# Seven block products in place of eight in two of the eight chunks of the gate and up projections

## The chip, the cores and the metric

One core of one Trainium2 chip runs the whole layer. The metric is the device time of one execution in microseconds (us). Engines are named as in the profile: PE (TensorE, matmuls; PEld is its weight load), DVE (VectorE), ACT (ScalarE), POOL (GpSimd), SP (SyncE, which issues most DMAs).

## The reference

The reference is a one-layer encoder trunk on 256 tokens of width 2048 in float32: four mixers with gates, an output projection, and a SwiGLU feed-forward with norms around each part. The change touches the feed-forward alone:

```
h = rms_norm(x, norm_ffn_pre[l])                                        # 256 x 2048
ffn = (jax.nn.silu(h @ w_gate[l]) * (h @ w_up[l])) @ w_down[l]          # 2048 -> 5632 -> 2048
x = x + rms_norm(ffn, norm_ffn_post[l])
```

## The kernel before

A float32 product is made as three products in the fp32r type. Each operand is split into a rounded part hi and a rest lo, and the kernel adds hi x hi, hi x lo and lo x hi. The activations are split once (`h2_hi`, `h2_lo`, features on partitions, 16 k tiles of 128 features x 256 tokens). The weights are split as they arrive.

The weights are streamed in chunks of 256 features x 512 columns (512 KB). `Stream.chunk` (L588 to L602) loads a chunk by a DMA of SP into a `raw` tile (4 buffers, L592 and L593), ACT rounds it into `hi` (L600), and DVE subtracts to get `lo` (L601); `hi` and `lo` have 3 buffers each. These instructions carry a high scheduling priority, so they run as far ahead of the matmuls as the buffers allow.

`gemm_tok` (L646 to L664) multiplies 256 tokens by 512 columns. It goes through eight chunks; for each of a chunk's two k tiles and two halves of 128 tokens it issues three matmuls (L661 to L663), with the tokens as the stationary operand and 512 weight columns as the moving one. That makes 12 matmuls of 512 columns per chunk and 96 per projection, which accumulate in two PSUM banks. `gemm_feat` (L669 to L683), used earlier in the layer and not touched, is the other way round: its matmuls move 256 columns.

The feed-forward goes through 11 pairs (loop over `g`, L1019): a gate projection, a sigmoid on ACT and a product on DVE for each token half (L1025, L1026), an up projection, a product of the two on DVE (L1029), eight transposes on PE into `tq` (L1034), and two copies to `aT` on ACT (L1035). After the pairs comes the down projection (L1039 to L1088). Its activations are split per chunk into `ah` on ACT (L1044) and `al` on DVE (L1045), three buffers each, and its matmuls are L1056 to L1058. Half of its PSUM banks come from a pool `wd`, opened after the pool `tq` is closed (L1036). `ah`, `al`, `fg`, `sq` and `gain` lie in the pool `F`, which is open from before the first pair. The row of gains for the last norm is loaded by a DMA of POOL before the first pair (L1017).

The program is traced in this order and then scheduled by the framework: each engine gets one queue in order, by priority and by the framework's own estimate of when operands are ready, and semaphores are put where an operand or a buffer is needed. Engines carry out their queues in order.

Of the kernel before, what the change touches and what calls it, by code (L numbers as in the profile page):

```python
# [581 lines left out]
class Stream:  # L582


    def __init__(self, e, ring):
        self.e, self.ring = e, ring
# [18 lines left out]
def hybrid_kernel(tc, x, xt, w_l, w_in, w_branch, w_out, w_gate, w_up, w_down, post_mix, post_ffn, wa2_d, w2_d, a2_d, g2_d, lq_d,  # L605
                  vec_d, cst_d, lev_d, out):
    from contextlib import ExitStack
    nc = tc.nc
    V, S, G, T = nc.vector, nc.scalar, nc.gpsimd, nc.tensor
    e = Env()  # L610
    e.tc, e.nc = tc, nc
    e.boost, e.mix, e.nraw, e.nhi = 200000, 100000, 4, 3
    mm = T.matmul

    with ExitStack() as ctx:
        base = ctx.enter_context(tc.tile_pool(name="base", bufs=1))
        ring = ctx.enter_context(tc.tile_pool(name="ring", bufs=1))
# [2 lines left out]
        e.dram = ctx.enter_context(tc.tile_pool(name="dr", bufs=1, space=bass.MemoryType.DRAM))  # L620
        mmp = ctx.enter_context(tc.tile_pool(name="mmp", bufs=1, space=PSUM))
        stream = Stream(e, ring)

        def bank():
            return mmp.tile([128, 512], F32, tag="mm", name="mm", bufs=4)
# [15 lines left out]
        def rms(ssum, n, eps):  # L641

            V.tensor_scalar(ssum, ssum, 1.0 / n, eps, op0=ALU.mult, op1=ALU.add)  # L643
            G.tensor_tensor(ssum, ssum, e.mhalf.to_broadcast(list(ssum.shape)), op=ALU.pow)

        def gemm_tok(w, lhs, nk, banks, runs={}, into={}):  # L646
# [92 lines left out]
        with ExitStack() as mctx:  # L739
# [54 lines left out]
            with ExitStack() as rctx:  # L794
# [32 lines left out]
                for q, c0 in (("l", None), ("k", COL["rk"]), ("r", COL["rr"]), ("v", COL["rv"])):  # L827
# [4 lines left out]
                    if q == "l":  # L832
# [3 lines left out]
                        o = VCOL["w0"][0]  # L836
# [40 lines left out]
            with ExitStack() as sctx:  # L877
# [6 lines left out]
                k = e.M.tile([128, 2, 256], F32, tag="m2", name="k")  # L884
# [5 lines left out]
                for c in range(2):  # L890
                    t = e.M.tile([128, 2, 512], F32, tag="m4", name="vg")
# [121 lines left out]
        with ExitStack() as fctx:  # L1013
            F = fctx.enter_context(tc.tile_pool(name="F", bufs=1))
            aT = F.tile([128, 44, 256], F32, name="aT")
            gain = F.tile([128, 2048], F32, name="gain2")
            nc.gpsimd.dma_start(gain, post_ffn.unsqueeze(0).to_broadcast([128, 2048]))  # L1017
            with tc.tile_pool(name="tq", bufs=1, space=PSUM) as tq:
                for g in range(11):  # L1019
                    bg, bu = [bank(), bank()], [bank(), bank()]  # L1020
                    lhs2 = lambda kt: (h2_hi[:, kt], h2_lo[:, kt])
                    sg = F.tile([128, 2, 512], F32, tag="sg", name="sg", bufs=2)
                    gemm_tok(columns(w_gate, g), lhs2, 16, bg, {0: 3} if g == 0 else {})
                    for i in range(2):
                        S.activation(sg[:, i], bg[i], AF.Sigmoid, scale=r2[:, i, 0:1])  # L1025
                        V.scalar_tensor_tensor(sg[:, i], bg[i], r2[:, i, 1:2], sg[:, i], op0=ALU.mult, op1=ALU.mult)  # L1026
                    gemm_tok(columns(w_up, g), lhs2, 16, bu)
                    for i in range(2):
                        V.tensor_tensor(sg[:, i], sg[:, i], bu[i], op=ALU.mult)  # L1029
                    for kp in range(2):  # L1030
                        ps = tq.tile([128, 2, 256], F32, tag="tq", name="tq", bufs=4)
                        for k in range(2):
                            for i in range(2):
                                T.transpose(ps[:, k, i * 128:(i + 1) * 128], sg[:, i, (2 * kp + k) * 128:(2 * kp + k + 1) * 128], ident)  # L1034
                        S.copy(aT[:, 4 * g + 2 * kp:4 * g + 2 * kp + 2], ps)  # L1035
            wd = fctx.enter_context(tc.tile_pool(name="wd", bufs=1, space=PSUM))  # L1036
            fg = F.tile([128, 2, 2048], F32, name="fg")
            sq = F.tile([128, 512], F32, name="sqf", bufs=2)
            for hf in range(2):  # L1039
                bk = [[(bank() if j == 0 else wd.tile([128, 512], F32, tag="wd", name="wd", bufs=4)) for i in range(2)] for j in range(2)]  # L1040
                def activations(kc):
                    ah = F.tile([128, 2, 256], F32R, tag="ah", name="ah", bufs=3)
                    al = F.tile([128, 2, 256], F32R, tag="al", name="al", bufs=3)
                    S.copy(ah, aT[:, 2 * kc:2 * kc + 2])  # L1044
                    V.tensor_tensor(al, aT[:, 2 * kc:2 * kc + 2], ah.bitcast(F32), op=ALU.subtract)  # L1045
                    return ah, al

                def chunk(kc, j, into=None):
                    return stream.chunk(w_down[kc, 2 * hf + j], 512, into)

                def products(kc, a, ch, j, i):
                    (ah, al), (hi, lo) = a, ch
                    ts = slice(i * 128, (i + 1) * 128)
# [36 lines left out]
            for i in range(2):  # L1090
                with tc.high_priority(offset=e.boost):
                    V.tensor_reduce(s1[:, i:i + 1], ssq[:, i], axis=AX.X, op=ALU.add)
                    rms(s1[:, i:i + 1], 2048.0, 1e-6)
                for g in range(4):
                    cs = slice(g * 512, (g + 1) * 512)
                    V.scalar_tensor_tensor(fg[:, i, cs], fg[:, i, cs], s1[:, i:i + 1], x2[:, i, cs], op0=ALU.mult, op1=ALU.add)
                    (nc.sync, nc.scalar)[g % 2 * i].dma_start(outr[:, i, cs], fg[:, i, cs])


class TagPool:  # L1100
# [67 lines left out]
```

## Time and profile before

| | us |
|---|---|
| median of 3 runs (1647.34 to 1647.59) | 1647.38 |
| profiled execution | 1646.67 |
| its span, first to last instruction | 1644.9 |
| granted clock of TensorE, mean | 0.999 |

The span is 1.8 us shorter than the profiled execution's own time, and that execution is 0.7 us under the median. In the rows further down, each time is that of one instruction or a sum over a group; a matmul's duration is its latency, and matmuls are pipelined, so the spacing of their starts is what a matmul costs. A row of busy times by engine has them in the order PE, PEld, DVE, ACT, POOL, each with its number of instructions.

### The profile page before, as it was taken

What the parts mean: (1) busy time and instruction counts of PE and PEld (TensorE: products, weight loads), DVE (VectorE), ACT (ScalarE), POOL (GpSimd) and SP (SyncE); (2) the same over time, 40 slices, a digit from 0 to 9 for tenths busy, and PEclk for the clock granted to TensorE, in tenths of its full rate; (3) what the DMA queues carried; (4) which work ended last, traced back from release to release, by engine and by line L of the source; (5) the groups of instructions that cost most, each with busy time, mean ns of one, the idle gap of its engine ahead of it and who ended that gap; (6) DMA issues with size and microseconds to landing.
All of it is one profiled execution on the core that took longest, in us unless ns stands there. A gap on an engine that the chain in (4) does not pass through costs nothing.

```text
span 1644.9 us, 21807 instructions
## 1 busy us (share of the span) xinstructions
PE 1630.8 (99%) x8632; PEld 1384.4 (84%) x8632; DVE 996.1 (61%) x1173; ACT 759.8 (46%) x879; POOL 33.1 (2%) x46
## 2 busy tenths in 40 slices
PE   9999999999999999999999999999999999999997
PEld 8999988887889978888888888888888888888886
DVE  7668785669875477555555755554455555556555
ACT  5453443336554355444444644444444444445443
POOL 0000110000000001000000000000000000000000
PEclk9999999999999999999999999999999999999999
DMA  8554665445556555765556555555555555555654
GB/s 293 185 165 147 185 209 173 139 141 166 167 166 193 185 161 181 268 192 190 184 190 204 191 187 188 191 192 188 187 189 190 192 192 190 184 198 187 202 192 141
DMA packets 85974, 306.84 MB, mean 187 GB/s; under 512 B 9584, under 2 KB 11904, under 8 KB 85360
## 3 DMA queue, kind: packets, MB, share of 16 engines
q1 hardware_dynamic: 84208, 298.72, 55.7%
q0 software_dynamic: 1232, 5.95, 1.2%
q8 instruction: 67, 1.10, 0.3%
q10 hardware_dynamic: 432, 0.79, 0.2%
q14 instruction: 35, 0.29, 0.0%
HBM read 302.40 MB, written 3.01 MB: 186 GB/s over the span
## 4 chain that ended last, share of the span: by engine, by line
PE 97%; DVE 1%; issue 1%; DMA 0%; ACT 0%; POOL 0%; DVEq 0%; POOLq 0%; ACTq 0%
PE mm L662 21%; PE mm L663 21%; PE mm L661 21%; PE mm L683 5%; PE mm L682 4%; PE mm L681 4%; PE mm L1056 2%; PE mm L1058 2%; PE mm L1057 2%; PE wd L1058 2%; PE wd L1057 2%; PE wd L1056 2%; PE tq L1034 1%; DVE lo L601 0%; PE ps L465 0%
## 5 line engine op out<-in xcount | busy, mean ns | idle before, releaser
L601 DVE TENSOR_TENSOR lo<-raw,hi 128x1024 fp32r<-128x1024 f32 (+1 forms) x554 | 677.1, 1223 | 552.7 <-ACT hi L600 552.0
L600 ACT CAST hi<-raw 128x1024 fp32r<-128x1024 f32 (+1 forms) x554 | 582.4, 1052 | 725.4 <-PE mm L663 508.4
L662 PE MATMUL mm<-lo,h_hi 128*128 128x512 f32 x704 | 274.9, 390 | 0.0
L663 PE MATMUL mm<-hi,h_lo 128*128 128x512 f32 x704 | 273.9, 390 | 0.1
L661 PE MATMUL mm<-hi,h_hi 128*128 128x512 f32 x704 | 250.6, 391 | 0.2 <-ACT h_hi L361 0.2
L662 PE MATMUL mm<-lo,hT_hi 128*128 128x512 f32 x608 | 238.7, 393 | 0.2 <-DVE lo L601 0.2
L663 PE MATMUL mm<-hi,hT_lo 128*128 128x512 f32 x608 | 237.6, 391 | 0.0
L661 PE MATMUL mm<-hi,hT_hi 128*128 128x512 f32 x608 | 219.7, 392 | 1.9 <-ACT vg L895 1.9
L681 PE MATMUL mm<-hT_hi,hi 128*128 128x256 f32 (+1 forms) x640 | 180.5, 284 | 0.1
L682 PE MATMUL mm<-hT_lo,hi 128*128 128x256 f32 (+1 forms) x640 | 179.8, 282 | 0.7 <-DVE hT_lo L362 0.7
L683 PE MATMUL mm<-hT_hi,lo 128*128 128x256 f32 (+2 forms) x640 | 178.7, 282 | 1.1 <-DVE lo L601 1.1
L661 PEld LDWEIGHTS mm<-hi,h_hi 128*128 128x128 f32 x704 | 132.2, 188 | 27.8 <-ACT h_hi L361 0.9
L663 PEld LDWEIGHTS mm<-hi,h_lo 128*128 128x128 f32 x704 | 132.2, 188 | 27.6 <-DVE s L643 0.5
L662 PEld LDWEIGHTS mm<-lo,h_hi 128*128 128x128 f32 x704 | 132.2, 188 | 27.0
L661 PEld LDWEIGHTS mm<-hi,hT_hi 128*128 128x128 f32 x608 | 114.2, 188 | 26.3 <-ACT vg L895 2.3
L662 PEld LDWEIGHTS mm<-lo,hT_hi 128*128 128x128 f32 x608 | 114.2, 188 | 25.1 <-issue 1.0
L663 PEld LDWEIGHTS mm<-hi,hT_lo 128*128 128x128 f32 x608 | 114.2, 188 | 23.7 <-issue 0.3
L682 PEld LDWEIGHTS mm<-hT_lo,hi 128*128 128x128 f32 (+1 forms) x640 | 121.0, 189 | 1.8 <-DVE hT_lo L362 0.9
L681 PEld LDWEIGHTS mm<-hT_hi,hi 128*128 128x128 f32 (+1 forms) x640 | 119.6, 187 | 1.6 <-issue 0.5
L683 PEld LDWEIGHTS mm<-hT_hi,lo 128*128 128x128 f32 (+2 forms) x640 | 119.0, 187 | 2.0 <-DVE lo L601 1.5
L1058 PE MATMUL mm<-hi,al 128*128 128x512 f32 x168 | 65.4, 389 | 0.0
L1057 PE MATMUL mm<-lo,ah 128*128 128x512 f32 x168 | 65.4, 389 | 0.0
(361 smaller groups left out, 1671.2 us busy)
## 6 DMA issues: line engine op xcount, KB each, us to landing
raw<-in_w_in_dram SPq DMA_DIRECT2D x224, 512.0 KB, 3.7
raw<-in_w_gate_dram SPq DMA_DIRECT2D x88, 512.0 KB, 3.5
raw<-in_w_up_dram SPq DMA_DIRECT2D x88, 512.0 KB, 3.5
raw<-in_w_down_dram SPq DMA_DIRECT2D x88, 512.0 KB, 3.5
raw<-in_w_branch_dram SPq DMA_DIRECT2D x32, 512.0 KB, 4.1
raw<-in_w_out_dram SPq DMA_DIRECT2D x32, 512.0 KB, 3.5
raw<-in_w_l_dram SPq DMA_DIRECT2D x8, 464.0 KB, 6.9
xs<-in_x_dram POOLq DMA_DIRECT2D x1, 2048.0 KB, 13.2
```

The lines of the kernel that those rows point to most:

```text
L600: nc.scalar.copy(hi[:, :, :w], raw[:, :, :w])
L601: nc.vector.tensor_tensor(lo[:, :, :w], raw[:, :, :w], hi[:, :, :w].bitcast(F32), op=ALU.subtract)
L661: mm(banks[i_], ah[:, ts], hi[:, k, :], start=kt == 0, stop=False)
L662: mm(banks[i_], ah[:, ts], lo[:, k, :], start=False, stop=False)
L663: mm(banks[i_], al[:, ts], hi[:, k, :], start=False, stop=kt == nk - 1)
L681: mm(ps, hi[:, k, cs], hT_hi[:, kt, :], start=first, stop=False, skip_group_check=True)
L682: mm(ps, hi[:, k, cs], hT_lo[:, kt, :], start=False, stop=False, skip_group_check=True)
L683: mm(ps, lo[:, k, cs], hT_hi[:, kt, :], start=False, stop=last, skip_group_check=True)
L1034: T.transpose(ps[:, k, i * 128:(i + 1) * 128], sg[:, i, (2 * kp + k) * 128:(2 * kp + k + 1) * 128], ident)
L1056: mm(bk[j][i], ah[:, k, ts], hi[:, k, :], start=kt == 0, stop=False)
L1057: mm(bk[j][i], ah[:, k, ts], lo[:, k, :], start=False, stop=False)
L1058: mm(bk[j][i], al[:, k, ts], hi[:, k, :], start=False, stop=kt == 43)
```

## The change

For pairs 1 to 10, `gemm_seven` takes the place of `gemm_tok`. Chunks 0, 1, 3, 4, 6 and 7 go on as before. Chunks 2 and 5 are seen as a 2 x 2 by 2 x 2 block product (two token halves, two k tiles, two column halves of 256), which is done with seven block products after Winograd in place of eight: 21 matmuls of 256 columns in place of 12 of 512. Three of the seven products go straight into the two banks of the projection, four into two more banks, `px` and `py`.

The sums of activations that this needs are made once, during the first pair (`sums`: POOL adds, ACT and DVE split). The sums of weights are made for each such chunk by three additions on DVE, and the seven weight blocks are split by two ACT copies and two DVE subtractions into `hi7` and `lo7` (2 buffers each). After the projection `close` adds up the results: one ACT copy and five DVE additions into a tile `w7` in SBUF, from which the sigmoid and the products then read. The three additions that need only `px` and `py` don't need the projection's last chunks; the last two add its banks.

The pool `tq` has 2 buffers in place of 4. The tiles of the seven products lie in a pool `U`, open during the pairs only. `gain` and its DMA, `fg`, `sq`, `ah` and `al` move to a pool `F2`, which is opened after `U` is closed.

```diff
+        def gemm_seven(w, lhs, banks, seven):
+            px, py = seven.banks()
+            for kc in range(8):
+                if kc in seven.kcs:
+                    seven.products(kc, lhs, seven.chunk(w(kc)), banks, px, py, kc == seven.kcs[0])
+                    continue
+                hi, lo = stream.chunk(w(kc))
...
+            with tc.high_priority(offset=e.boost):
+                return seven.close(banks, px, py)
...
-            gain = F.tile([128, 2048], F32, name="gain2")
-            nc.gpsimd.dma_start(gain, post_ffn.unsqueeze(0).to_broadcast([128, 2048]))
-            with tc.tile_pool(name="tq", bufs=1, space=PSUM) as tq:
+            with tc.tile_pool(name="U", bufs=1) as U, tc.tile_pool(name="tq", bufs=1, space=PSUM) as tq:
+                seven = Seven(e, U, tq, (2, 5))
...
+                    if g == 0:
+                        gemm_tok(columns(w_gate, g), lhs2, 16, bg, {0: 3})
+                        zg = bg
+                        seven.sums(h2_hi, h2_lo)
+                    else:
+                        zg = gemm_seven(columns(w_gate, g), lhs2, bg, seven)
...
-                        ps = tq.tile([128, 2, 256], F32, tag="tq", name="tq", bufs=4)
+                        ps = tq.tile([128, 2, 256], F32, tag="tq", name="tq", bufs=2)
...
+            F = fctx.enter_context(tc.tile_pool(name="F2", bufs=1))
+            gain = F.tile([128, 2048], F32, name="gain2")
+            nc.gpsimd.dma_start(gain, post_ffn.unsqueeze(0).to_broadcast([128, 2048]))
...
+    def sums(self, h_hi, h_lo):
+        e, nc = self.e, self.e.nc
+        G = nc.gpsimd
+        for c, kc in enumerate(self.kcs):
...
+            G.tensor_tensor(h, h_hi[:, 2 * kc:2 * kc + 2].bitcast(F32), h_lo[:, 2 * kc:2 * kc + 2].bitcast(F32), op=ALU.add)
...
+            G.tensor_tensor(s[:, 0], a21, a22, op=ALU.subtract)
...
+            nc.scalar.copy(self.s_hi[:, c], s)
+            nc.vector.tensor_tensor(self.s_lo[:, c], s, self.s_hi[:, c].bitcast(F32), op=ALU.subtract)
+    def chunk(self, ap):
+        e, nc = self.e, self.e.nc
+        G = nc.vector
+        with e.tc.high_priority(offset=e.boost):
+            raw = e.ring.tile([128, 2, 512], F32, tag="raw", name="raw", bufs=e.nraw)
+            nc.sync.dma_start(raw, ap)
+            b = raw.rearrange("p k (c n) -> p (k c) n", c=2)
+            t = self.pool.tile([128, 4, 256], F32, tag="t", name="t", bufs=2)
+            G.tensor_tensor(t[:, 0:2], b[:, 1:3], b[:, 0:1].to_broadcast([128, 2, 256]), op=ALU.add)
+            G.tensor_tensor(t[:, 2], t[:, 0], b[:, 2], op=ALU.add)
+            G.tensor_tensor(t[:, 3], t[:, 2], b[:, 3], op=ALU.add)
...
+            for x, o in ((b[:, 1:4], slice(0, 3)), (t, slice(3, 7))):
+                nc.scalar.copy(hi[:, o], x)
+                nc.vector.tensor_tensor(lo[:, o], x, hi[:, o].bitcast(F32), op=ALU.subtract)
+        return hi, lo
+    def products(self, kc, lhs, ch, banks, px, py, first):
...
+        for (ah, al), b, ps, st in ((a(0, 0), 0, px[:, 0], first), (s(1), 5, px[:, 1], False), (s(2), 4, py[:, 0], first),
+                                    (s(0), 3, py[:, 1], False), (a(1, 0), 2, banks[0][:, 256:512], False),
+                                    (s(3), 1, banks[0][:, 0:256], False), (a(1, 1), 6, banks[1][:, 256:512], False)):
+            mm(ps, ah, hi[:, b], start=st, stop=False, skip_group_check=True)
+            mm(ps, ah, lo[:, b], start=False, stop=False, skip_group_check=True)
+            mm(ps, al, hi[:, b], start=False, stop=kc == self.kcs[-1], skip_group_check=True)
+    def close(self, banks, px, py):
...
+        nc.scalar.copy(w[:, 2], px[:, 0])
+        V.tensor_tensor(w[:, 0], w[:, 2], px[:, 1], op=ALU.add)
+        V.tensor_tensor(w[:, 4], w[:, 0], py[:, 0], op=ALU.add)
+        V.tensor_tensor(w[:, 1:4:2], py[:, 1:2].to_broadcast([128, 2, 256]), w[:, 0:5:4], op=ALU.subtract)
+        out = []
+        for i in range(2):
+            o = w[:, 1 + 2 * i:3 + 2 * i].rearrange("p b n -> p (b n)")
+            V.tensor_tensor(o, o, banks[i], op=ALU.add)
+            out.append(o)
+        return out
```

## Rows read from the trace of the kernel before

**Rows 1.** The page: busy time of each engine, then the chain that ended last.
```profile
PE 1630.8 (99%) x8632; PEld 1384.4 (84%) x8632; DVE 996.1 (61%) x1173; ACT 759.8 (46%) x879; POOL 33.1 (2%) x46
...
PE 97%; DVE 1%; issue 1%; DMA 0%; ACT 0%; POOL 0%; DVEq 0%; POOLq 0%; ACTq 0%
```

**Rows 2.** Pairs 2 to 10: length, then busy by engine, clock, DMA share, GB/s.
```profile
1025.00:1370.00 345.00, 345.00 (x1555) 286.10 (x1554) 171.47 (x155) 147.69 (x155) 0.00 (x0) 1.00 0.58 189
```

**Rows 3.** Waits in 1025 to 1370 us: who, for whom, total, times, longest.
```profile
ACT hi L600 <- PE mm L663: 177.8, 110, 1.7
DVE lo L601 <- ACT hi L600: 171.5, 125, 2.6
```

**Rows 4.** PE timeline, 512 columns: start, duration; a row with x2 is two.
```profile
199.84 0.39 PE L663 MATMUL mm<-hi,hT_lo 128*128 128x512 f32 x1
...
205.96 0.39 PE L663 MATMUL mm<-hi,hT_lo 128*128 128x512 f32 x1
```

**Rows 5.** PE timeline, 256 columns, in `gemm_feat`: start, duration.
```profile
519.72 0.28 PE L682 MATMUL mm<-hT_lo,hi 128*128 128x256 f32 x1
...
522.90 0.28 PE L682 MATMUL mm<-hT_lo,hi 128*128 128x256 f32 x1
```

**Rows 6.** The last pair's end and the down projection's start: DVE, ACT, PE.
```profile
1394.42 1.23 DVE L601 TENSOR_TENSOR lo<-raw,hi 128x1024 fp32r<-128x1024 f32 x1 [1.49 <-ACT hi L600]
1395.56 1.28 DVE L1029 TENSOR_TENSOR sg<-sg,mm 128x512 f32<-128x512 f32 x2
...
1399.73 1.07 ACT L1035 COPY aT<-tq 128x512 f32<-128x512 f32 x2
...
1395.62 0.39 PE L663 MATMUL mm<-hi,h_lo 128*128 128x512 f32 x1
...
1398.58 1.04 PE L1034 MATMUL tq<-ident,sg 128*128 128x128 f32 x8
1399.37 0.71 PE L1056 MATMUL mm<-hi,ah 128*128 128x512 f32 x2
```

**Rows 7.** DVE timeline: additions and subtractions of several sizes, and their starts.
```profile
218.18 0.41 DVE L252 TENSOR_TENSOR NN<-NN,tmp 64x252 f32<-64x252 f32 x1
218.62 0.41 DVE L250 TENSOR_TENSOR tmp<-D,NN 64x247 f32<-64x247 f32 x1
...
393.79 0.69 DVE L426 SCALAR_TENSOR_TENSOR h<-h,s 128x512 f32<-128x512 f32 x1
394.51 0.69 DVE L427 SCALAR_TENSOR_TENSOR x<-h,x 128x512 f32<-128x512 f32 x1
```

**Rows 8.** One chunk's split in pair 2, on ACT and then DVE.
```profile
1037.84 1.05 ACT L600 CAST hi<-raw 128x1024 fp32r<-128x1024 f32 x1 [1.66 <-PE mm L663]
...
1038.92 1.23 DVE L601 TENSOR_TENSOR lo<-raw,hi 128x1024 fp32r<-128x1024 f32 x1 [1.49 <-ACT hi L600]
```

**Rows 9.** Pool `L` handed over to `F`: `L`'s last DVE read of `ssq`, POOL's DMA.
```profile
926.71 0.15 DVE L1008 TENSOR_REDUCE r<-ssq 128x1 f32<-128x4 f32 x1
...
927.51 0.58 POOL L1017 DMA_DIRECT2D gain<-in_post_ffn_dram  x1 [21.76 <-PE mm L663]
```

**Rows 10.** POOL: a memset, and the widest arithmetic that it does.
```profile
L245 POOL MEMSET NN<- x1: 977/977/977, 183.6 to 183.6; 64x1024 f32 x1
...
L159 POOL TENSOR_TENSOR rn<-rn,mhalf x1: 2912/2912/2912, 127.4 to 127.4; 128x16 f32<-128x16 f32 x1
```

**Rows 11.** Pool `R` handed over to `S1`: DVE, then PE.
```profile
369.28 1.22 DVE L353 TENSOR_TENSOR oT<-BV,oT 128x1024 fp32r<-128x1024 f32 x1
370.53 0.69 DVE L887 SCALAR_TENSOR_TENSOR q<-mm,rB 128x512 f32<-128x512 f32 x1
...
369.34 0.39 PE L663 MATMUL mm<-hi,hT_lo 128*128 128x512 f32 x1
371.62 0.50 PE L661 MATMUL mm<-hi,hT_hi 128*128 128x512 f32 x1 [1.89 <-ACT vg L895]
```

**Rows 12.** `ah` on ACT, down projection: durations ns min/median/max, starts.
```profile
L1044 ACT CAST ah<-aT x44: 610/624/633, 958.2 to 1619.8; 128x512 fp32r<-128x512 f32 x44
```

More of the change, by code (lines that the diff above doesn't have):

```diff
@@ L622, in hybrid_kernel @@
         stream = Stream(e, ring)
+        e.ring = ring
         def bank():
@@ L644, in rms @@
             G.tensor_tensor(ssum, ssum, e.mhalf.to_broadcast(list(ssum.shape)), op=ALU.pow)
+        def gemm_seven(w, lhs, banks, seven):
[5 more added lines that the diff above has]
+                hi, lo = stream.chunk(w(kc))
+                for k in range(2):
+                    kt = 2 * kc + k
+                    ah, al = lhs(kt)
+                    for i in range(2):
+                        ts = slice(i * 128, (i + 1) * 128)
+                        mm(banks[i], ah[:, ts], hi[:, k, :], start=kt == 0, stop=False, skip_group_check=True)
+                        mm(banks[i], ah[:, ts], lo[:, k, :], start=False, stop=False, skip_group_check=True)
+                        mm(banks[i], al[:, ts], hi[:, k, :], start=False, stop=kt == 15, skip_group_check=True)
+            with tc.high_priority(offset=e.boost):
+                return seven.close(banks, px, py)
         def gemm_tok(w, lhs, nk, banks, runs={}, into={}):
@@ L1015, in hybrid_kernel @@
             aT = F.tile([128, 44, 256], F32, name="aT")
[L1016 to L1018 removed]
+            lhs2 = lambda kt: (h2_hi[:, kt], h2_lo[:, kt])
+            with tc.tile_pool(name="U", bufs=1) as U, tc.tile_pool(name="tq", bufs=1, space=PSUM) as tq:
+                seven = Seven(e, U, tq, (2, 5))
                 for g in range(11):
                     bg, bu = [bank(), bank()], [bank(), bank()]
[L1021 removed]
                     sg = F.tile([128, 2, 512], F32, tag="sg", name="sg", bufs=2)
[L1023 to L1027 removed]
+                    if g == 0:
[4 more added lines that the diff above has]
+                        zg = gemm_seven(columns(w_gate, g), lhs2, bg, seven)
+                    for i in range(2):
+                        S.activation(sg[:, i], zg[i], AF.Sigmoid, scale=r2[:, i, 0:1])
+                        V.scalar_tensor_tensor(sg[:, i], zg[i], r2[:, i, 1:2], sg[:, i], op0=ALU.mult, op1=ALU.mult)
+                    if g == 0:
+                        gemm_tok(columns(w_up, g), lhs2, 16, bu)
+                        zu = bu
+                    else:
+                        zu = gemm_seven(columns(w_up, g), lhs2, bu, seven)
                     for i in range(2):
[L1029 removed]
+                        V.tensor_tensor(sg[:, i], sg[:, i], zu[i], op=ALU.mult)
                     for kp in range(2):
[L1031 removed]
+                        ps = tq.tile([128, 2, 256], F32, tag="tq", name="tq", bufs=2)
                         for k in range(2):
@@ L1097, in hybrid_kernel, with __init__, banks @@
                     (nc.sync, nc.scalar)[g % 2 * i].dma_start(outr[:, i, cs], fg[:, i, cs])
+class Seven:
+    def __init__(self, e, pool, psum, kcs):
+        self.e, self.pool, self.psum, self.kcs = e, pool, psum, kcs
+        n = len(kcs)
+        pad = lambda name, w: pool.tile([128, w], F32R, name=name)
+        self.s_hi, self.s_lo = (pad(n_, 4 * 128 * n).rearrange("p (c b t) -> p c b t", c=n, b=4) for n_ in ("s_hi", "s_lo"))
+    def sums(self, h_hi, h_lo):
[3 more added lines that the diff above has]
+            t = self.pool.tile([128, 4, 256], F32, tag="t", name="t", bufs=2)
+            h, s = t[:, 0:2], t[:, 2:4].rearrange("p x (b t) -> p (x b) t", t=128)
+            G.tensor_tensor(h, h_hi[:, 2 * kc:2 * kc + 2].bitcast(F32), h_lo[:, 2 * kc:2 * kc + 2].bitcast(F32), op=ALU.add)
+            a11, a21, a12, a22 = h[:, 0, 0:128], h[:, 0, 128:256], h[:, 1, 0:128], h[:, 1, 128:256]
+            G.tensor_tensor(s[:, 0], a21, a22, op=ALU.subtract)
+            G.tensor_tensor(s[:, 2], a11, a21, op=ALU.subtract)
+            G.tensor_tensor(s[:, 1], s[:, 0], a11, op=ALU.subtract)
+            G.tensor_tensor(s[:, 3], a12, s[:, 1], op=ALU.add)
+            nc.scalar.copy(self.s_hi[:, c], s)
+            nc.vector.tensor_tensor(self.s_lo[:, c], s, self.s_hi[:, c].bitcast(F32), op=ALU.subtract)
+    def banks(self):
+        return [self.psum.tile([128, 2, 256], F32, tag=n, name=n, bufs=1) for n in ("px", "py")]
+    def chunk(self, ap):
[5 more added lines that the diff above has]
+            b = raw.rearrange("p k (c n) -> p (k c) n", c=2)
+            t = self.pool.tile([128, 4, 256], F32, tag="t", name="t", bufs=2)
+            G.tensor_tensor(t[:, 0:2], b[:, 1:3], b[:, 0:1].to_broadcast([128, 2, 256]), op=ALU.add)
+            G.tensor_tensor(t[:, 2], t[:, 0], b[:, 2], op=ALU.add)
+            G.tensor_tensor(t[:, 3], t[:, 2], b[:, 3], op=ALU.add)
+            hi, lo = (self.pool.tile([128, 1920], F32R, tag=n, name=n, bufs=2)[:, 48:1840].rearrange("p (b n) -> p b n", n=256)
+                      for n in ("hi7", "lo7"))
+            for x, o in ((b[:, 1:4], slice(0, 3)), (t, slice(3, 7))):
[3 more added lines that the diff above has]
+    def products(self, kc, lhs, ch, banks, px, py, first):
+        mm = self.e.nc.tensor.matmul
+        hi, lo = ch
+        c = self.kcs.index(kc)
+        a = lambda k, i: tuple(x[:, i * 128:(i + 1) * 128] for x in lhs(2 * kc + k))
+        s = lambda b: (self.s_hi[:, c, b], self.s_lo[:, c, b])
+        for (ah, al), b, ps, st in ((a(0, 0), 0, px[:, 0], first), (s(1), 5, px[:, 1], False), (s(2), 4, py[:, 0], first),
[5 more added lines that the diff above has]
+    def close(self, banks, px, py):
+        nc = self.e.nc
+        V = nc.vector
+        w = self.pool.tile([128, 5, 256], F32, tag="w7", name="w7", bufs=1)
+        nc.scalar.copy(w[:, 2], px[:, 0])
[3 more added lines that the diff above has]
+        out = []
+        for i in range(2):
+            o = w[:, 1 + 2 * i:3 + 2 * i].rearrange("p b n -> p (b n)")
+            V.tensor_tensor(o, o, banks[i], op=ALU.add)
+            out.append(o)
+        return out
```

## Prediction

> **What bounds the kernel now.** I read the engines' busy shares first: PE is busy 99% of the span, DVE 61%, ACT 46%, and 97% of the chain that ended last runs on PE [rows 1]. In the stretch that the change touches this is sharper: between pairs 2 and 10 PE is busy all the time, at full clock, DVE half of it and ACT 43%, with the DMAs at 0.58 [rows 2]. The waits say the same from the other side: ACT waits for matmuls to give a buffer back, DVE waits for ACT [rows 3], and nobody else. So the pairs take the time in which PE issues its matmuls. What a matmul costs there is the spacing of starts and not its duration. Between the two rows of 512 columns lie 27 steps in 6.12 us: 0.2267 us each [rows 4]. For 256 columns there are 27 steps in 3.18 us: 0.1178 us each [rows 5]. The weight loads hide behind both.
>
> **The change, part by part.**
>
> *Matmuls.* A chunk was 12 x 0.2267 = 2.720 us; with seven products it is 21 x 0.1178 = 2.474 us, 0.247 us less. Ten pairs, two projections, two chunks make 40 such chunks: 9.9 us less on PE. That an eighth of the work brings 9% of the time is due to the fixed part of a matmul, which is now paid 21 times in place of 12. The rows of 256 columns have weights as the stationary operand and tokens as the moving one, the new matmuls the reverse; both are 128x128 against 128x256, so I take the row. The Trainium skill's page "TensorE: Matmul & The Clock Gate" (section "Wait — 56ns, not 53.3ns?") puts a warm matmul at its columns over 2.4 GHz plus 2.5 ns. By that the saving would be 11.8 us (an estimate from that page); the trace has 13 ns over the columns at 512 and 11 ns at 256, and the sum goes by the trace.
>
> *Weights on DVE and ACT.* Starts of independent DVE instructions stand 1.14 us apart behind one of 1024 elements [rows 6] and about 0.60 behind one of 512 (1.28 for two, each 0.68) [rows 6]; where the second needs the first, 0.72 for 512 and 0.44 for about 256 [rows 7]. For 768 no row exists; it lies between 0.60 and 1.14, and I take the middle, 0.87. A seven-product chunk then costs DVE 0.72 + 0.44 + 0.44 for the sums and 0.87 + 1.14 for the two `lo`: 3.61 us in place of 1.14. The five additions of `close` cost 0.44 + 0.44 + 0.72 + 0.60 + 0.60 = 2.80 us. A pair on DVE: 12 x 1.14 + 4 x 3.61 + 2 x 2.80, two products after the sigmoid at 0.72 and two with the up projection at 0.60: 36.4 us. PE needs 144 x 0.2267 + 84 x 0.1178 + 0.79 for the transposes (1398.58 to 1399.37 [rows 6]) = 43.3 us. So DVE goes from half to 84% and stays under PE; ACT, at 1.05 for 1024 elements [rows 8], comes to some 24 us. I cost this at nothing as long as the order in the queues hides it. The cover: ACT starts a chunk's `hi` when PE is done with the chunk three before it; `lo` ends 2.3 us later [rows 8], and PE gets there after two more chunks, 5.4 us. Some 3 us are to spare, and a seven-product chunk between adds 2.5 us to that, for `hi7` and `lo7` have buffers of their own. If the cover is gone, each us late on DVE is one on PE. Bounds: 0 to 0.7 us per projection (worked out with the rivals); I take 0.5 us in all.
>
> *DMAs.* The same chunks go in the same order through SP; a `raw` buffer of a seven-product chunk is held some 2.5 us longer, until the sums and the second `lo` are done. The transfers take 0.58 of the DMA engines' time [rows 2], and ACT, their first reader, waits for matmuls and not for them [rows 3]. Nothing is added.
>
> *Sums of activations.* Ten POOL instructions, with two ACT copies and two DVE subtractions, have from 927, where POOL is free for them [rows 9], to about 958: ten pairs of 44.3 us back from the start of the down projection at 1395.85, and two chunks on. POOL's rows are a memset of 1024 elements in 0.98 us and a power of 16 elements in 2.9 us [rows 10]; the sums are 2048 elements, so 2 us by the first and 370 us by the second. An addition is nearer to the memset: hidden. The far end stays as a small chance.
>
> *The handover to the down projection.* This is the edit that I price highest. `ah` and `al` used to lie in a pool of their own time; now their pool is opened where `U` was. What the trace shows of such handovers: the first write in `S1` starts 0.03 us after the last read in `R` ended (369.28 + 1.22 = 370.50), and PE stood 1.89 us [rows 11]; POOL's load for `F` was held until `L`'s last read had ended at 926.86 [rows 9]. A new pool waits for the whole of the old one. The last reader of `U` is the product of the last pair (L1029 before), which reads `w7`. So: last up matmul starts at 0, ends at 0.39; two additions of the banks and two products on DVE, 3 x 0.60 + 0.68; `ah` 0.62 [rows 12]; some 0.15 for the steps between engines: PE starts the down projection at 3.64, where it started one step of 0.23 behind [rows 4, 6], 3.4 us late. The eight transposes, 0.79 us, fall into that gap and come off the work behind it: 2.6 us lost. Low end 0, if memory is handed over piece by piece; high end 4.8, if a `lo` (1.14) and the two copies to `aT` (1.07 [rows 6]) stand ahead in the queues. `gain` is late by the same, but is needed only after half of the down projection; the `wd` banks wait as they did.
>
> *The end of each up projection.* The transposes now come 1.2 us later, after two more additions. PE has the next gate projection to do meanwhile; before, they were 1.7 us behind the ready products (1396.84 to 1398.58 [rows 6]).
>
> Sum against the profiled execution: 1646.67 - 9.9 + 2.6 + 0.5 = 1639.9. The median lies 0.7 above that execution, so the time predicted is 1640.6.
>
> **The rivals.**
>
> *DVE's queue is late (slower).* DVE does its queue in order. If in each projection one `lo` that PE needs stands behind a whole seven-product chunk, 3.61 us against 2.9 to spare, PE waits 0.7 us: 20 x 0.7 = 14 us, and the time is 1640.1 + 14 = 1654. It decides from 0.36 us per projection (gain gone) and 0.53 (slower). For it: DVE at 84%, with bursts where `close`, the sigmoid's products and a seven-product chunk meet; each wait of DVE for a bank or for ACT comes off the 7 us per pair that are left. Against it: chunk 2's work can be done as soon as its weights have landed, long before its turn. The same skill page ("Architectural detail: the array is 16× 32×32, not 1× 128×128") calls the queues of ScalarE and VectorE strictly first in, first out, which is what this rival lives on; the trace agrees, with DVE's waits in front of `lo` [rows 3].
>
> *Partly late.* The same at 0.2 to 0.5 us per projection, or the transposes of each pair waiting for the longer chain on DVE: 4 to 10 us back, 1644 to 1650.
>
> *Handover for nothing.* If `ah` can be written while PE is on the last two chunks, 2.6 us come back: 1638. Against it, both handovers of the trace.
>
> *The sums on POOL hold up ACT's queue* in the first pair: by the power's rate hundreds of us. I see no reason for it.
>
> **How the numbers follow.** Forecast 0.50, handover for nothing 0.12, partly late 0.18, DVE's queue 0.19, POOL 0.01. A measurement of this kernel tells 0.2%, 3.3 us, from no change. The first two are faster: 0.62. Partly late counts as the same: 0.18. The rest is slower: 0.20. The range goes from 1636.8, the handover for nothing and a little more, to 1653, which leaves out about half of the slow case and the far end. The likeliest case alone: 1638 to 1643.5.
>
> **What would show it.** In the profile after: starts 0.118 us apart in the seven-product chunks, and PE without waits in pairs 2 to 10, each pair 1.0 us shorter; DVE busy about 85% there. Matmuls further apart than 0.125 would make the first step wrong; PE waits for `lo` or `lo7` within the pairs would show the DVE rival; PE waits behind the transposes the partial one. Between the last up matmul and the first of the down projection PE should stand about 2.6 us beside the transposes, waiting for `ah`; if it goes on at once, the handover step is wrong. A result above 1647 would make the prediction wrong as a whole.

## The result and the profile after

The changed kernel takes 1664.34 us (median of four runs, 1663.09 to 1665.88) against 1647.36 for the kernel before on the same chip: a ratio of 1.0107, with a 95% interval of 1.0095 to 1.012. It is slower by 17 us; 6.8 us less was forecast, and the time lies outside the range.

Lines of the changed kernel, as far as they occur below: `hi` and `lo` of ordinary chunks L600 and L601, their load L593, `gemm_seven`'s 512-column matmuls L660 to L662; of a seven-product chunk the load L1169, the three weight sums L1172 to L1174, `hi7` and `lo7` L1178 and L1179, the 256-column matmuls L1192 to L1194; `close` L1201 to L1208; the products after the up projection L1057, the transposes L1062, the down projection L1087 to L1089.

The page of the changed kernel, busy time by engine and then the chain that ended last, against [rows 1]:

```profile
PE 1626.8 (98%) x8992; PEld 1393.6 (84%) x8992; DVE 1125.0 (68%) x1435; ACT 789.6 (48%) x941; POOL 42.1 (3%) x56
...
PE 74%; DVE 10%; DMA 10%; issue 5%; ACT 1%; POOL 0%; DVEq 0%; POOLq 0%; ACTq 0%; SPq 0%
```

A tenth of the chain is now DVE and a tenth DMA, where 97% was PE. Pairs 2 to 10, against [rows 2]:

```profile
1025.00:1370.00 345.00, 327.90 (x1743) 281.33 (x1742) 257.31 (x340) 160.95 (x191) 0.00 (x0) 1.00 0.55 181
```

PE is idle for 17 of 345 us. DVE has 257 us of work, far from full, and the DMAs' share has fallen from 0.58 to 0.55: nothing here is short of capacity. The waits in 1020 to 1370 us (total, times, longest), against [rows 3]:

```profile
ACT hi L1178 <- DMA raw<-in_w_gate_dram: 56.7, 16, 5.1
ACT hi L1178 <- DMA raw<-in_w_up_dram: 52.4, 14, 4.7
DVE t L1172 <- DMA raw<-in_w_up_dram: 49.7, 14, 5.5
...
DVE t L1172 <- DMA raw<-in_w_gate_dram: 34.2, 16, 3.7
...
PE mm L661 <- DVE lo L601: 10.6, 7, 2.6
...
PE tq L1062 <- DVE sg L1057: 6.5, 11, 1.0
```

In the kernel before no engine waited for a weight load there. Now ACT and DVE do, both at the first instruction of a seven-product chunk, and PE waits for DVE in two places. I added up how far starts on PE stand beyond 0.227, 0.118 or 0.09 us (512, 256 and 128 columns), where it is more than 0.05 us, between 900 and 1420 us: 32.2 us, against 3.5 before. Of it 13.5 stand ahead of a matmul with an ordinary `lo`, and 13.2 ahead of transposes, 2.1 of these at the handover to the down projection. So 28.7 us are new: less the 9.9 forecast for the matmuls that is +18.8. The two profiled executions differ by only 16.4, since the feed-forward's first matmul starts at 901.45 us here and at 904.25 before (903.8 to 905.2 in all versions below), 2.8 us earlier in code that the change does not touch; why is not shown. From that matmul to the last of the down projection the changed kernel takes 750.9 us against 731.6, 19.3 more, so the sum closes to 0.5 us.

How a load makes PE wait is seen in pair 3. DVE first (start, duration, what ended the idle time):

```profile
1048.18 1.22 DVE L601 TENSOR_TENSOR lo<-raw,hi 128x1024 fp32r<-128x1024 f32 x1
1053.50 0.69 DVE L1172 TENSOR_TENSOR t<-raw 128x512 f32<-128x512 f32 x1 [4.10 <-DMA raw<-in_w_up_dram]
1054.11 1.22 DVE L601 TENSOR_TENSOR lo<-raw,hi 128x1024 fp32r<-128x1024 f32 x1
...
1063.04 0.69 DVE L1172 TENSOR_TENSOR t<-raw 128x512 f32<-128x512 f32 x1 [2.52 <-DMA raw<-in_w_up_dram]
1063.65 1.22 DVE L601 TENSOR_TENSOR lo<-raw,hi 128x1024 fp32r<-128x1024 f32 x1
```

ACT, which made the `hi` that the subtraction at 1054.11 needs:

```profile
1049.58 1.05 ACT L600 CAST hi<-raw 128x1024 fp32r<-128x1024 f32 x1 [0.65 <-PE mm L662]
```

SP's queue, which issued the two loads:

```profile
1049.43 0.33 SPq L1169 DMA_DIRECT2D raw<-in_w_up_dram  x1
...
1058.03 0.33 SPq L1169 DMA_DIRECT2D raw<-in_w_up_dram  x1
```

PE, at the second of these sums:

```profile
1064.92 0.50 PE L661 MATMUL mm<-lo,h_hi 128*128 128x512 f32 x1 [1.03 <-DVE lo L601]
```

The `hi` was ready at 1050.63, but its `lo` began at 1054.11, because a weight sum stood ahead of it in DVE's queue, and that sum waited 4.10 us for its load. The load was issued at 1049.43, as soon as the `lo` of 1048.18 had given back its `raw` tile, and took some 4 us to land. The second time the spare time of `lo` is used up, and PE stands.

The transposes wait for the same queue, late in another way. Those of this pair, on PE:

```profile
1090.24 0.44 PE L1062 MATMUL tq<-ident,sg 128*128 128x128 f32 x2 [0.51 <-DVE sg L1057]
...
1091.98 0.87 PE L1062 MATMUL tq<-ident,sg 128*128 128x128 f32 x6 [0.60 <-DVE sg L1057]
```

DVE there: a `lo` that is late stands between the two products that the transposes need.

```profile
1089.51 0.68 DVE L1057 TENSOR_TENSOR sg<-sg,w 128x512 f32<-128x512 f32 x1
1090.11 1.22 DVE L601 TENSOR_TENSOR lo<-raw,hi 128x1024 fp32r<-128x1024 f32 x1
1091.24 0.68 DVE L1057 TENSOR_TENSOR sg<-sg,w 128x512 f32<-128x512 f32 x1
```

The handover, against [rows 6] and [rows 11], on PE:

```profile
1409.80 0.39 PE L662 MATMUL mm<-hi,h_lo 128*128 128x512 f32 x1
1411.67 0.44 PE L1062 MATMUL tq<-ident,sg 128*128 128x128 f32 x2 [1.48 <-DVE sg L1057]
1412.27 0.88 PE L1062 MATMUL tq<-ident,sg 128*128 128x128 f32 x6 [0.17 <-DVE sg L1057]
1413.02 0.47 PE L1087 MATMUL mm<-hi,ah 128*128 128x512 f32 x1
```

From the last up matmul to the first of the down projection are 3.22 us, 0.79 of which is the transposes and 0.23 the usual step: 2.2 us lost, with the same addition, product and `ah` on the way as worked out before.

### The profile page after: what moved, and what is told of

The parts are those of the page before. It is cut to its first block, busy times and chain, and to the rows that moved or that the text cites. A ratio compares the mean times of both kernels' runs of the same rounds, so it can differ in the third digit from the quotient of the medians.

```text
span 1661.3 us, 22825 instructions
## 1 busy us (share of the span) xinstructions
PE 1626.8 (98%) x8992; PEld 1393.6 (84%) x8992; DVE 1125.0 (68%) x1435; ACT 789.6 (48%) x941; POOL 42.1 (3%) x56
## 4 chain that ended last, share of the span: by engine, by line
PE 74%; DVE 10%; DMA 10%; issue 5%; ACT 1%; POOL 0%; DVEq 0%; POOLq 0%; ACTq 0%; SPq 0%
PE mm L682 13%; PE mm L683 12%; PE mm L681 12%; DMA raw<-in_w_up_dram 6%; DVE lo L601 5%; PE mm L703 4%; PE mm L702 4%; PE mm L701 4%; DMA raw<-in_w_gate_dram 4%; PE mm L1087 2%; PE mm L1089 2%; PE mm L1088 2%; PE wd L1087 2%; PE wd L1088 2%; PE wd L1089 2%
## 5 line engine op out<-in xcount | busy, mean ns | idle before, releaser
L601 DVE TENSOR_TENSOR lo<-raw,hi 128x1024 fp32r<-128x1024 f32 (+1 forms) x514 | 626.3, 1220 | 340.8 <-ACT hi L600 340.3
L600 ACT CAST hi<-raw 128x1024 fp32r<-128x1024 f32 (+1 forms) x514 | 538.4, 1049 | 524.1 <-PE mm L683 281.2
L661 PE MATMUL mm<-lo,h_hi 128*128 128x512 f32 x480 | 188.4, 392 | 11.9 <-DVE lo L601 11.9
L662 PE MATMUL mm<-hi,h_lo 128*128 128x512 f32 x480 | 187.6, 391 | 0.0
L660 PE MATMUL mm<-hi,h_hi 128*128 128x512 f32 x480 | 183.9, 390 | 0.0
L661 PEld LDWEIGHTS mm<-lo,h_hi 128*128 128x128 f32 x480 | 90.3, 188 | 30.2 <-DVE lo L601 13.5
L662 PEld LDWEIGHTS mm<-hi,h_lo 128*128 128x128 f32 x480 | 90.3, 188 | 18.2
L660 PEld LDWEIGHTS mm<-hi,h_hi 128*128 128x128 f32 x480 | 90.2, 188 | 17.4
L1178 ACT CAST hi<-raw 128x768 fp32r<-128x768 f32 x40 | 33.4, 836 | 133.5 <-DMA raw<-in_w_up_dram 68.0
L1172 DVE TENSOR_TENSOR t<-raw 128x512 f32<-128x512 f32 x40 | 27.7, 692 | 101.9 <-DMA raw<-in_w_up_dram 64.8
```

What stands on the lines that cost most here:

```text
L600: nc.scalar.copy(hi[:, :, :w], raw[:, :, :w])
L601: nc.vector.tensor_tensor(lo[:, :, :w], raw[:, :, :w], hi[:, :, :w].bitcast(F32), op=ALU.subtract)
L660: mm(banks[i], ah[:, ts], hi[:, k, :], start=kt == 0, stop=False, skip_group_check=True)
L661: mm(banks[i], ah[:, ts], lo[:, k, :], start=False, stop=False, skip_group_check=True)
L662: mm(banks[i], al[:, ts], hi[:, k, :], start=False, stop=kt == 15, skip_group_check=True)
```

## The experiments

My theory from here on: the work fits, its order does not. The sums of a seven-product chunk stand ahead of ready work while their load is still on the way. The rivals: DVE has too much to do; the transposes, or the handover, are what is lost; too few buffers for loads.

**The matmuls alone (b_mm256).** The kernel before, with only the 21 matmuls of 256 columns in chunks 2 and 5 of pairs 1 to 10, on the ordinary `hi` and `lo`. It leaves out an eighth of these chunks' products.

```diff
+                        if c in seven:
+                            for n in range(7):
+                                k, i_, cs = n // 4, n // 2 % 2, slice(n % 2 * 256, n % 2 * 256 + 256)
...
+                                mm(banks[i_][:, cs], ah[:, ts], hi[:, k, cs], start=False, stop=False, skip_group_check=True)
...
```

> The kernel before, with nothing changed but the matmuls of chunks 2 and 5 in pairs 1 to 10: 21 of 256 columns from the ordinary hi and lo in place of 12 of 512 (an eighth of these two chunks is left out of the sums). It measures the saving on PE alone. If a matmul of 256 columns costs 0.118 us here as in gemm_feat, the time is 9.9 us under before, 1637.5 us. If the reversed operands make it dearer, it is 1642 or more. If the finer issue brings waits of its own, PE shows them in the pairs.

Measured: 1639.17 us, a ratio of 0.9952 (0.9937 to 0.9967), 8.2 us less. The first transposes of pairs 1 and 9, on PE of this kernel:

```profile
999.85 0.39 PE L1043 MATMUL tq<-ident,sg 128*128 128x128 f32 x2
...
1349.51 0.39 PE L1043 MATMUL tq<-ident,sg 128*128 128x128 f32 x2
```

That is 43.71 us a pair; the same two starts before were 1000.67 and 1356.17, 44.44 a pair. So a pair gains 0.73 us where 0.99 was forecast: the 256-column starts stand 0.1197 apart on average here, not 0.1178, which is 0.16 of the 0.26 us that are missing. The saving is real and most of its size was right.

**Own load buffers (a_raw7), the transposes later (a_late), no weight sums (a_nosum).** Each is the changed kernel with one edit, after which the scheduler orders the queues anew. `a_late` traces a pair's transposes behind the next gate projection. `a_nosum` leaves out the three sums, so that four of seven blocks use other weights.

```diff
 # a_raw7
-            raw = e.ring.tile([128, 2, 512], F32, tag="raw", name="raw", bufs=e.nraw)
+            raw = self.pool.tile([128, 2, 512], F32, tag="raw7", name="raw7", bufs=2)
 # a_late
...
+                    while pending:
+                        to_aT(*pending.pop())
...
+                    pending.append((g, sg))
 # a_nosum
-            G.tensor_tensor(t[:, 0:2], b[:, 1:3], b[:, 0:1].to_broadcast([128, 2, 256]), op=ALU.add)
-            G.tensor_tensor(t[:, 2], t[:, 0], b[:, 2], op=ALU.add)
-            G.tensor_tensor(t[:, 3], t[:, 2], b[:, 3], op=ALU.add)
...
-            for x, o in ((b[:, 1:4], slice(0, 3)), (t, slice(3, 7))):
+            for x, o in ((b[:, 1:4], slice(0, 3)), (b, slice(3, 7))):
```

> The changed kernel, with two load buffers of their own for the seven-product chunks (in the pool U), so that their DMA no longer waits for one of the four shared raw buffers. Theory A, late landing: DVE's first sum of such a chunk is at the head of DVE's queue and waits 1.4 to 4.5 us for the weights, with lo of ordinary chunks ready behind it; the loads are late since a shared buffer comes free only when DVE has done the chunk four before. Then DVE's waits for DMA (102 us) fall to under 30, PE's waits for lo (13 us) go, and the time falls by 10 to 20 us, to 1645 to 1654. Theory B, DVE has too much to do in the pairs (its load alone): it stays within 3 us of 1664.

> The changed kernel, with the transposes of a pair (and its copies to aT) traced after the next pair's gate projection, so that they stand about 20 us later in PE's queue. If the waits of PE in front of the transposes (13 us in the pairs) are a loss of their own, they go and the time is 1651 to 1654. If they only stand in for DVE being late, PE waits for lo instead and the time is above 1659.

> The changed kernel without the three weight sums on DVE (four of the seven weight blocks are then wrong ones; the splits stay, as do all matmuls and loads): 1.6 us less of DVE work in each of 40 chunks, 64 us in all. Theory B, DVE's load: both kinds of PE waits go, 1638 to 1645. Theory A, late landing: lo7 and ACT's hi7 still wait for the same late weights with ordinary chunks behind them, and the time stays above 1652.

Measured: `a_raw7` 1650.2 us (ratio 1.0016, 1.0007 to 1.0026), `a_late` 1669.36 (1.0136, 1.0121 to 1.0151), `a_nosum` 1670.4 (1.0142, 1.0127 to 1.0157). The waits of `a_nosum` in 1020 to 1370 us:

```profile
DVE lo L1175 <- ACT hi L1174: 115.4, 30, 6.0
ACT hi L1174 <- DMA raw<-in_w_up_dram: 67.6, 15, 5.7
ACT hi L1174 <- DMA raw<-in_w_gate_dram: 66.8, 15, 6.0
...
PE tq L1062 <- DVE sg L1057: 13.6, 7, 3.9
```

Without the sums DVE has 222.75 us of work in 1025 to 1370 in place of 257.31, and the kernel is no faster: `hi7` waits for the load in ACT's queue, and DVE for `hi7`. This speaks against the theory that DVE is overloaded, with a reservation: the second part of `hi7` and `lo7` is made from `raw` itself here, which holds a `raw` tile longer, and SP waited 108.4 us in this stretch for `lo7` to be done with one. `a_issue` below settles it. The waits of `a_raw7` in the same stretch:

```profile
DVE t L1172 <- DMA raw<-in_w_up_dram: 37.2, 16, 3.7
DVE t L1172 <- DMA raw<-in_w_gate_dram: 27.5, 15, 2.6
...
PE tq L1062 <- DVE sg L1057: 7.0, 14, 1.2
```

With buffers of its own the load is no longer held by the ring, PE's waits for `lo` are gone, and 14 us come back; how much of that is the buffers and how much the new order in the queues, this run does not tell. But the sums still wait 65 us for loads, and the transposes still wait as before. In `a_late` the transposes no longer wait in the pairs; the waits for `lo` grow from 13.5 to 21.7 us. Moving the transposes moves the loss.

**Combinations (a_late_raw7, a_raw7_hi, a_all1).** `a_late_raw7` joins the two edits. `a_raw7_hi` gives `close` and the products L1057 twice the scheduling priority. `a_all1` is `a_late_raw7` with one `raw7` buffer, and `ah` and `al` as in the next experiment.

```diff
 # a_raw7_hi, beside a_raw7's edit
-            with tc.high_priority(offset=e.boost):
+            with tc.high_priority(offset=2 * e.boost):
                 return seven.close(banks, px, py)
...
+                    with tc.high_priority(offset=2 * e.boost):
```

> Load buffers of their own for the seven-product chunks, and the transposes traced after the next gate projection, together. Alone, the first gave 1650.2 us with PE's waits for lo gone and 12.8 us of waits in front of the transposes left (about 2 of them at the handover to the down projection), and the second 1669.4 us, for PE then waited for lo. Theory A: with the loads in time the transposes' wait is the last loss in the pairs, and moving them takes it away: 1638 to 1642 us. Rival, DVE is behind by itself: the wait turns up at lo again, and the time is 1648 or more.

> Load buffers of their own, and the closing additions and the products with the up projection at a higher scheduling priority than the splitting of chunks, so that they go ahead of it in DVE's queue. If the transposes wait since chunk work stands between these on DVE (0.6 to 1.2 us between the two products of a pair), the waits in front of them fall from 10.7 us in the pairs to under 4, and the time to 1640 to 1645. If the chain of two additions and two products is too long by itself, it stays at 1649 to 1651.

> All together: one load buffer of its own for the seven-product chunks (no room for two), the transposes after the next gate projection, ah and al in the earlier pool with two buffers each. Theory A with one buffer enough: the matmuls' saving is kept, 1637 to 1640, as the matmuls alone gave 1639.2. If one buffer is too few, DVE waits for the load again, with PE's waits for lo back, and it is 1645 or more.

Measured: 1648.68 (1.0008, 0.9998 to 1.0018), 1649.98 (1.0018, 1.0008 to 1.0027) and 1649.37 (1.0013, 1.0003 to 1.0022). I had expected several us more from each. With the transposes out of the way, 9.8 and 6.8 us of waits for `lo` came back; with the higher priority the transposes still waited 11.6 us. A sum that waits at the head of the queue keeps back whatever comes next; which work that is seems not to matter.

**The handover alone (a_ah2).** `ah` and `al`, two buffers each, go back to the pool of their former lifetime.

```diff
-                    ah = F.tile([128, 2, 256], F32R, tag="ah", name="ah", bufs=3)
-                    al = F.tile([128, 2, 256], F32R, tag="al", name="al", bufs=3)
+                    ah = FA.tile([128, 2, 256], F32R, tag="ah", name="ah", bufs=2)
+                    al = FA.tile([128, 2, 256], F32R, tag="al", name="al", bufs=2)
```

> The changed kernel, with ah and al in the pool that is open from before the pairs, as in the kernel before (two buffers each, for room): the handover alone undone. If a new pool waits for the whole of the old one, PE's pause before the down projection (2.0 us in front of the last transposes) goes, and ah is written before the last products of the last pair; in the time that is 2 us of 1664, less than its runs differ by. If the pause is due to the transposes alone, it stays.

Measured, in one run: 1667.54 us. PE goes from the up projection straight to the down projection:

```profile
1414.61 0.39 PE L661 MATMUL mm<-lo,h_hi 128*128 128x512 f32 x1
...
1415.06 0.39 PE L1088 MATMUL mm<-hi,ah 128*128 128x512 f32 x1
```

The gap there is gone (two usual steps between these rows), so the pool was its cause, and the waits in the pairs are as they were (14.6 us ahead of `lo`, 12.5 ahead of transposes, by the spacing). The total of this single run is no better. Part of the reason is at the end of the kernel. The last row of DVE's final products in `a_ah2`, and the last matmul:

```profile
1655.09 0.39 PE L1090 MATMUL wd<-wl,al 128*128 128x512 f32 x1
...
1659.67 2.74 DVE L1128 SCALAR_TENSOR_TENSOR fg<-fg,s1f,acc 128x512 f32<-128x512 f32 x4 [0.67 <-POOL s1f L645]
```

The same two in the changed kernel:

```profile
1652.35 0.39 PE L1089 MATMUL wd<-wl,al 128*128 128x512 f32 x1
...
1655.24 2.74 DVE L1127 SCALAR_TENSOR_TENSOR fg<-fg,s1f,acc 128x512 f32<-128x512 f32 x4 [0.67 <-POOL s1f L645]
```

From the last matmul to the last products are 4.58 us in place of 2.89: with another order both token halves are finished behind the last matmul, where one was begun before it. That takes 1.7 of the 2.1 us back. The feed-forward also began 2.6 us later than in the changed kernel's profiled execution (904.08 us against 901.45), and the stretch from there to the last up matmul is 2.4 us longer.

**The order alone (a_issue, a_raw7_issue).** Nothing is removed, resized or given more room: the sums and splits of a seven-product chunk are put behind the `hi` and `lo` of the chunk before in the queues of ACT and DVE. `a_raw7_issue` has two own load buffers beside that. The line below makes the order; lines not shown hand it the two instructions.

```diff
...
-        with e.tc.high_priority(offset=e.boost):
+        with e.tc.high_priority(offset=e.boost), e.tc.issue_after(INS(stream.hi_ins)), e.tc.issue_after(INS(stream.lo_ins)):
```

> The changed kernel, with the four shared load buffers as they are; only the order in the queues is changed: the sums and splits of a seven-product chunk stand behind the split of the chunk before it, on DVE and on ACT, so that ready ordinary work no longer waits behind a sum whose weights have not landed. Theory A1, the order does the harm: DVE's and ACT's waits for DMA (102 and 134 us) fall to under a third and the time to 1643 to 1652. Theory A2, the shared buffers do it (a load can't be issued until a seven-product chunk lets go of its buffer): the waits move but PE still waits, 1656 or more.

> Load buffers of their own and the changed order together. Load buffers alone left 1650.2 us, with 66 us of DVE waits for DMA and the transposes late. If what is left is the order (a sum that waits for its load stands ahead of the closing additions), the waits in front of the transposes fall from 10.7 us in the pairs to under 4: 1640 to 1644. If the transposes are late for the length of the chain alone, 1648 to 1651.

Measured: `a_issue` 1642.28 us (ratio 0.9974, 0.9963 to 0.9985), `a_raw7_issue` 1643.04 (0.9975, 0.9964 to 0.9986). The edit takes the kernel from 1.0107 to 0.9974, and buffers of their own bring nothing beside it. SP issues the loads in the same sequence as in the changed kernel. Pairs 2 to 9 of `a_issue`:

```profile
1020.00:1360.00 340.00, 339.93 (x1843) 294.24 (x1842) 275.99 (x360) 177.91 (x203) 0.00 (x0) 1.00 0.58 194
```

PE does not wait, and DVE is busier than in the slow kernel, 81%: the theory that it has too much to do falls with this. DVE of `a_issue`, where the changed kernel had its second wait above (L1176 is the first sum here):

```profile
1059.89 1.22 DVE L601 TENSOR_TENSOR lo<-raw,hi 128x1024 fp32r<-128x1024 f32 x1 [1.24 <-ACT hi L600]
1061.03 0.68 DVE L1176 TENSOR_TENSOR t<-raw 128x512 f32<-128x512 f32 x1
```

The ordinary `lo` goes first, and the sum finds its weights there.

**Loads from another queue (a_raw7_q).** Own buffers as in `a_raw7`, and the loads of seven-product chunks issued by POOL, not SP; the order on DVE is left to the scheduler.

```diff
 # beside a_raw7's edit
-            nc.sync.dma_start(raw, ap)
+            nc.gpsimd.dma_start(raw, ap)
```

> Load buffers of their own, and the loads of the seven-product chunks issued from POOL's queue, which has nothing else to do in the pairs, in place of SP's, where they stand behind loads that wait for a shared buffer. If SP's order makes them late, DVE's waits for DMA fall from 66 us to under 20 and the time to 1640 to 1645. If they are late since several loads land together, in 5 us rather than 3.5, or POOL's own issue is slow, it stays at 1648 to 1652.

Measured: 1639.75 us (1639.68 to 1640.8) against 1646.57, a ratio of 0.996 (0.9945 to 0.9975): the lowest median of the versions that leave nothing out, and faster than both kernels. Its pairs, and the waits of DVE in 1020 to 1370 us:

```profile
1020.00:1360.00 340.00, 340.00 (x1853) 295.41 (x1853) 276.48 (x357) 175.42 (x202) 15.86 (x30) 1.00 0.61 193
```

```profile
DVE t L1172 <- DMA raw<-in_w_up_dram: 16.2, 9, 2.4
...
DVE t L1172 <- DMA raw<-in_w_gate_dram: 10.6, 8, 1.9
```

The sums' waits fall from 65 us to 27, no longer long enough to reach PE. I had expected that SP's queue held these loads back behind loads that wait for a shared buffer. The trace of `a_raw7` does not show that: between 1000 and 1380 us SP stood at each of the 32 such loads and waited for its own buffer.

```profile
SPq L1169 <- DVE lo L1179: 28.5, 32, 1.3
```

What did change with the edit is the order on DVE. The end of pair 3 in `a_raw7`, where a sum that waits stands ahead of the additions of the banks:

```profile
1086.54 0.69 DVE L1172 TENSOR_TENSOR t<-raw 128x512 f32<-128x512 f32 x1 [1.52 <-DMA raw<-in_w_up_dram]
1087.15 1.28 DVE L1208 TENSOR_TENSOR w<-w,mm 128x512 f32<-128x512 f32 x2
```

The same in `a_raw7_q`, where the additions go first and the sum finds its weights there:

```profile
1082.69 1.27 DVE L1208 TENSOR_TENSOR w<-w,mm 128x512 f32<-128x512 f32 x2
1083.96 0.69 DVE L1172 TENSOR_TENSOR t<-raw 128x512 f32<-128x512 f32 x1
1084.57 1.29 DVE L1057 TENSOR_TENSOR sg<-sg,w 128x512 f32<-128x512 f32 x2
```

These loads also land sooner, in 4.3 us in the median in place of 5.0. So the 9 us over `a_raw7` (0.996 against 1.0016 of the kernel before) are not shown to come from the queue of issue; this run does not tell it from the order and the landing. The Trainium skill ("Trainium Kernel Development and Optimization", section "Key Constraints") says that issuing DMAs from several engines saves only the sequencer's issue time. No run here shows it or speaks against it, since the order on DVE changed together with the queue.

**With the handover mended (a_issue_ah2, a_best_q).** `a_issue` and `a_raw7_q` with `a_ah2`'s edit; `a_best_q` has one `raw7` buffer, for want of space.

> The changed order in the queues (1642.3 us alone) with ah and al in the pool open from before the pairs, two buffers each. The handover then costs PE nothing. In the profile of the order alone PE stood 3.0 us in front of the last transposes, and the nine matmuls of 512 columns behind that were 0.427 us apart in place of 0.227, at half the granted clock: 1.8 us more. If that is what keeps it over the 1639.2 us of the matmuls alone, the time falls to 1637.5 to 1639.5 and its runs lie within 1 us of each other. If the closing chains in the pairs cost the rest, it stays above 1641.

> One load buffer of its own for the seven-product chunks, filled from POOL's queue, and ah and al in the earlier pool with two buffers each. With two buffers and the handover as changed it was 1639.75 us, with 2.1 us of PE's waits at the handover. If these go and one buffer is enough, 1637.2 to 1638.2. If one buffer is too few, PE waits for lo again and it is 1641 or more.

Measured: 1642.03 (0.997, 0.9958 to 0.9981) and 1644.32 (0.9984, 0.9975 to 0.9993); both above what I had hoped for. The end of the kernel is 1.7 us longer in both, as in `a_ah2`. In `a_issue_ah2` PE also stops a little later, for 1.45 us, for the copies of the last transposes, which stand behind a `hi` on ACT.

`a_best_q` loses another 2.5 us at pairs 0 and 1, where it waits for ordinary chunks. That accounts for most of its profiled execution's distance to `a_raw7_q`'s (1642.70 against 1639.82); that its median is another 1.6 us higher is not explained.

## Why the prediction was wrong

*The step that failed* is the one on DVE and ACT: "I cost this at nothing as long as the order in the queues hides it", taken at 0.5 us. The order did not hide it, and cost 22 us: 1664.34 us with it, 1642.28 with another. The sizes of this step were right. A `lo` of 768 was taken at 0.87 us, and the starts at 1055.58 and 1056.45 stand 0.87 apart. DVE's work was put at 36.4 us a pair and 84%; with the queues in a good order it is 276 of 340 us, 81%. But I asked only whether the work fits and how long each piece delays the next. The scheduler had put the sums ahead of ready `lo`s, and a queue that waits at its head for 4 us holds back everything: the "some 3 us to spare" went in the wait, not in the work. `a_issue` shows it by changing the order and nothing else; `a_nosum`, with its reservation, that less work in the same place does not help.

*The DMAs, "Nothing is added",* is the other half. It looked at the transfers' share, which fell. What mattered was when a load could be issued: a `raw` tile of a seven-product chunk is held until its sums and the `lo` made from it are done, SP issues in order, and the next load goes out when a tile comes free. Landing took 4.2 and 4.3 us in the median for gate and up, where it was 3.5 for both. I had seen that ACT did not wait for loads [rows 3], but that was with four tiles each held for a shorter time.

*The rival "DVE's queue is late"* had the direction, the engine and the strict order, and 1654 for the time. (Its own terms, 5.4 less 2.3, leave 3.1 us to spare and not the 2.9 it was priced with.) It had the wrong blocker: a whole chunk's work of 3.61 us, and not one addition of 0.69 that waits for a load. Against it I held that the work "can be done as soon as its weights have landed, long before its turn"; the trace shows the reverse, its turn came before its weights. "Partly late" described the transposes, which I had priced at nothing: 11 us, and a consequence, since they are gone in `a_issue`.

*What held:* the matmuls, with 8.2 us of 9.9 in `b_mm256`; the handover, 2.1 to 2.2 us of 2.6, and through the pool, as `a_ah2` shows; the sums on POOL, hidden, though POOL was busy 9.0 us longer (42.1 against 33.1) where 2 were reckoned. `a_raw7_q` comes to 6.8 us less than before (4.1 to 9.1 by the interval), which is what the sum had said, with parts not far from it: by the traces, 9.1 us less from the first matmul of the feed-forward to the last of the up projection, and 2.3 more from there to the last matmul, where 9.9 less and 3.1 more were forecast.

*What stays open:* why the scheduler put the sums first, which I did not try to find out; how much of the loss belongs to ACT's queue and how much to DVE's, since `a_issue` changed both; and what a queue of issue of its own is worth when the order stays as it is.

## What to carry to other kernels

Where a change adds work to an engine with a queue in order, ask for each new instruction what it waits for and what stands behind it, before asking whether the engine has time. Work that needs a fresh load belongs behind the work that is ready. Buffers of its own for the load brought 14 us here, the order brought 22, and both together no more than the order. An engine at 75% that holds up PE and an engine at 81% that does not are told apart by the waits in brackets, not by the busy share.

## What was not expected of the hardware

A stop of PE is sometimes paid twice. In the changed kernel, after the longest wait for a `lo`, by windows and on PE:

```profile
1158.00:1164.00 6.00, 5.02 (x19) 4.32 (x20) 6.00 (x9) 4.05 (x6) 0.00 (x0) 0.72 0.44 132
```

```profile
1158.98 0.50 PE L661 MATMUL mm<-lo,h_hi 128*128 128x512 f32 x1 [2.59 <-DVE lo L601]
...
1160.96 0.63 PE L660 MATMUL mm<-hi,h_hi 128*128 128x512 f32 x1
1161.39 0.63 PE L661 MATMUL mm<-lo,h_hi 128*128 128x512 f32 x1
```

For about 3 us the starts stand 0.43 us apart in place of 0.227, the lower of the clock's two levels, 1.2 GHz in place of 2.4; the granted clock of the window is 0.72. In the profiled execution of `a_issue` the handover had two stops, of 1.75 and 1.30 us. The clock in 1390 to 1400 us was 0.83, and nine matmuls of 512 columns behind the stops started 0.427 us apart, some 1.8 us more. After the changed kernel's own handover, with stops of 1.48 and 0.17 us, the clock stayed at full speed.
